# The last GpSimd products and sums of a hybrid diffusion backbone move to VectorE and ScalarE

## The chip, the core and the metric

The kernel runs on one core of a Trainium2 chip. The metric is the device time of one execution in microseconds (us); lower is better. A core has a matrix engine, TensorE (PE in the profile, with PEld for its weight loads), and three engines for the rest: VectorE (DVE), ScalarE (ACT) and GpSimd (POOL). SyncE (SP) issues DMAs, and so do the queues of ACT and POOL. Each engine executes its own queue in order; semaphores make it wait for the others.

## What is computed

One latent sequence and one context sequence of 256 tokens each, 2048 wide, fp32, go through two layers. The even layer runs 8 gated-DeltaNet heads (GDN) in both directions beside 8 neighbourhood-attention heads (NA); the odd layer is a gated short convolution; each is followed by a SwiGLU. The parts that the change touches, cut:

```python
def gated_delta_chunked(q, k, v, g, beta, s0):
    gc = jnp.cumsum(g, axis=-1)
    decay = jnp.exp(jnp.where(lower_incl, gc[..., :, None] - gc[..., None, :], -jnp.inf))
    m = jnp.where(i[:, None] > i[None, :], jnp.einsum('bhnid,bhnjd->bhnij', kb, k) * decay, 0.0)
    t_inv = lax.linalg.triangular_solve(eye + m, ...)
    ...                                        # scan over chunks with state s
def even_mixer(h, hc, ...):
    ka, va, kb, vb, a, b, qa, qb, za = split_segments(h @ w_in, EVEN_SEGS)
    ka, va, qa = short_conv_silu([ka, va, qa], conv_w)
    k_l = axial_rope(l2norm(heads(ka)))
    q_l = axial_rope(l2norm(heads(qa))) * HEAD_DIM ** -0.5
    o_l, _ = gdn_bidirectional(q_l, k_l, heads(va), g_l, beta_l, s_ctx_fin)
    y_gdn = rmsnorm(o_l, gdn_norm) * silu(za)
    y_na = neighbourhood_attention(qb, kb, vb, k_ctx_na, v_ctx_na, rpb)   # scores + rpb, masked
    return concatenate([y_gdn, y_na]) @ w_out
# every layer: x = x + gate * mixer(modulate(x)); x = x + gate * swiglu(modulate(x)); last: rmsnorm
```

## The kernel before

All weights stay in HBM and are streamed. `load_w` (L220) issues 512 KB loads on SP's queue; `split_w` (L229) makes of each 128x1024 block a rounded part whi on ACT (L168) and the rest wlo on DVE (L234); PE then does three products for each block (`tm_stream`, L273 to L276 and L282 to L284, with tokens in the rows; `fm_stream`, L298 and L302, with features in the rows and 256 columns per matmul). A stream that runs on time keeps PE busy; a whi or wlo that is late stops it.

The order of the streams in the even layer is: key blocks KA0 and KA1 (both sequences), query blocks QA0 and QA1, value blocks VA0 and VA1, then QB0 and QB1, KB and VB of the NA heads, and ZA. Between their matmuls stands the GDN work. A finished key, query or value block goes through `head_evac` (L550): a short convolution by four DVE taps and ACT's silu (cv, L535 to L548), transposes into out_t (hq), squares and their sums (L573 to L576). Then `normalise` (L587) scales and rotates keys and queries, and DMAs write them to kd, qTd and vd in HBM. `chunk_matrices` (L772) loads kd again as ktok, takes Gram matrices, multiplies with the exponentials that `decay` (L750) makes of gm, and solves 31 steps of small triangular systems on DVE (L825 and L827), ending in the copy lsol (L828), which goes out as dz (L834). `inverses` (L837 on) reads dz back as xd and xdT (L852) and puts the blocks together on PE (L868 on). `scan`, `latent_scores` (L970 on) and `latent_out` (L992 on) follow. For the NA heads, `na_scores` (L1060) loads a bias br (one buffer, two DMAs on ACT's queue), adds the mask in bq (L1072), takes scores on PE, their maximum on DVE (L1081), the exponential s on ACT (L1083) and the division on DVE (L1084, L1085); `na_values` uses s. Projections are copied by `stage` through nst (L1038) to HBM. `za_evac` (L1104) multiplies the gate with the norm's gain, `resid_evac` (L1134) adds a stream's result to the residual xs, with `norm_h` behind it. The pump's jobs (`ada_job`, L309) run beside all this: DVE sums 512-wide blocks of the modulation weights in acc (L321).

The program order of each engine is not that of the text: a scheduler reorders the instructions of all engines by its own model of their durations, so that a different engine for some operations also moves others.

Of the kernel before, what the change touches and what calls it, by code (L numbers as in the profile page):

```python
# [23 lines left out]
F32 = mybir.dt.float32  # L24
F32R = mybir.dt.float32r
AF = mybir.ActivationFunctionType
OP = mybir.AluOpType
# [77 lines left out]
def body(tc, x, c, ctx, c_ctx, ada_w, ada_b, norm_mix, norm_ffn, ffn_w_gate, ffn_w_up, ffn_w_down,  # L105
# [71 lines left out]
    def C(n):  # L177
        o, w = CO[n]
        return cs[:, o:o + w]
# [370 lines left out]
    def head_evac(n, q, c0, done, sums):  # L550

        st_ = {}

        def f(i_, p):
            st_[i_] = kvp.tile([128, 512], F32, name="hst", tag="hst", bufs=4)[:, 0:n * 128]
            copy(st_[i_], p[:, 0:n * 128])
            if i_ < 3:
                return
            out_t = kvp.tile([128, 4, 4, 128], F32, name="hq", tag="hq", bufs=2)
            ss = kvp.tile([128, 4, 4], F32, name="hss", tag="hss", bufs=2) if sums else None  # L560
            cvs = {}

            def front(i):
                cvs[i] = conv_silu(st_[i], n // 2, c0 + q * 4 + i)

            def back(i):
                pt = smt()
                for t in range(n):
                    ins = transpose(pt[:, t * 128:(t + 1) * 128], cvs[i][:, t * 128:(t + 1) * 128])
                    if not t:  # L570
                        tc.keep_in_program_order(ins)
                acopy(out_t[:, 0:n, i, :], pt[:, 0:n * 128].rearrange("p (t e) -> p t e", t=n))
                if sums:  # L573
                    sq = kvp.tile([128, 4, 128], F32, name="sq", tag="cv", bufs=CV)[:, 0:n, :]
                    POOL.tensor_tensor(sq, out_t[:, 0:n, i, :], out_t[:, 0:n, i, :], op=OP.mult)
                    DVE.tensor_reduce(ss[:, 0:n, i], sq, axis=AX.X, op=OP.add)  # L576


            for g_, i in ((front, 0), (front, 1), (front, 2), (back, 0), (front, 3), (back, 1), (None, 0), (back, 2), (back, 3)):
                if g_:  # L580
                    defer(g_, i)
                else:
                    defer(lambda: None)
            defer(done, out_t, ss)
        return f

    def normalise(xt, n, rs_):  # L587

        for t in range(n):
            xv = xt[:, t]  # L590
            POOL.tensor_tensor(xv, xv, rs_[:, t, :, None].to_broadcast([128, 4, 128]), op=OP.mult)
            if t < 2:
                x1, x2 = xv[:, :, 0:64], xv[:, :, 64:128]
                cb = cosT[:, None, t * 64:(t + 1) * 64].to_broadcast([128, 4, 64])
                sb = sinT[:, None, t * 64:(t + 1) * 64].to_broadcast([128, 4, 64])
                r = kvp.tile([128, 2, 4, 64], F32, name="rope", tag="rope", bufs=1)
                POOL.tensor_tensor(r[:, 0], x1, sb, op=OP.mult)
                POOL.tensor_tensor(r[:, 1], x2, sb, op=OP.mult)
                POOL.tensor_tensor(x1, x1, cb, op=OP.mult)
                POOL.tensor_tensor(x2, x2, cb, op=OP.mult)  # L600
                DVE.tensor_tensor(x1, x1, r[:, 1], op=OP.subtract)
                DVE.tensor_tensor(x2, x2, r[:, 0], op=OP.add)

# [146 lines left out]
    def decay(d, tt, q):  # L750

        gm = g2("gm")
        POOL.tensor_tensor(gm, C(("gt", "lt")[d])[:, None, :].to_broadcast([128, 4, 128]),
                           g_t[:, d, tt, q * 4:q * 4 + 4, None].to_broadcast([128, 4, 128]), op=OP.mult)
        pD = gdt()
        for i in range(4):
            PE.matmul(pD[:, i * 128:(i + 1) * 128], gm[:, i, :], C(("le", "ge")[d]), start=True, stop=True)
        em = g2("em")
        ACT.activation(em, pD.rearrange("p (i e) -> p i e", i=4), AF.Exp)
        return em  # L760
# [208 lines left out]
    def latent_scores(q):  # L969

        qT = load_feat("qT", qTd[:, q * 4:q * 4 + 4, :], lg, 1)
        kT = load_feat("kT", kTd[:, 0, q * 4:q * 4 + 4, :])
        AT = lg.tile([128, 16, 128], F32, name="AT", tag="AT", bufs=2)
        for ti in range(2):
            tok = slice(ti * 128, ti * 128 + 128)
            pK = gdt()
            for i in range(4):
                PE.matmul(pK[:, i * 128:(i + 1) * 128], kT[:, i, tok], qT[:, i, tok], start=True, stop=True)
            for d in range(2):
                em = decay(d, ti, q)  # L980
                POOL.tensor_tensor(em, em, C(("le", "ge")[d])[:, None, :].to_broadcast([128, 4, 128]), op=OP.mult)
                DVE.tensor_tensor(AT[:, d * 8 + ti * 4:d * 8 + ti * 4 + 4, :],
                                  pK.rearrange("p (i e) -> p i e", i=4), em, op=OP.mult)
        return AT
# [8 lines left out]
    def latent_out(q, o_t):  # L993
        zq = load_tok("vtok", zd.rearrange("p t (h e) -> p t h e", h=8), 0, q).rearrange("p t h e -> p t (h e)")
        sso = gw.tile([128, 2, 4], F32, name="sso", tag="sso", bufs=1)
        for t in range(2):
            sq = g2("osq")
            POOL.tensor_tensor(sq, o_t[:, t], o_t[:, t], op=OP.mult)
            DVE.tensor_reduce(sso[:, t], sq, axis=AX.X, op=OP.add)
        ro = rstd(gw, sso, [128, 2, 4], 8, HD, "ro")  # L1000
        for t in range(2):
            for i in range(4):
                DVE.scalar_tensor_tensor(o_t[:, t, i, :], o_t[:, t, i, :], ro[:, t, i:i + 1],
                                         zq[:, t, i * 128:(i + 1) * 128], op0=OP.mult, op1=OP.mult)
        for g in range(2):
            pt = gdt()
            for i in range(2):
                for t in range(2):
                    transpose(pt[:, i * 256 + t * 128:i * 256 + (t + 1) * 128], o_t[:, t, g * 2 + i, :])
            split(yhi[q][:, g * 2:g * 2 + 2, :], ylo[q][:, g * 2:g * 2 + 2, :], pt.rearrange("p (i e) -> p i e", i=2))  # L1010
# [50 lines left out]
    def na_scores(h):  # L1061
        kb = nap.tile([128, 512], F32, name="kb", tag="kb", bufs=2)
        qb = nap.tile([128, 256], F32, name="qb", tag="qb", bufs=2)
        bq = nap.tile([128, 6, 64], F32, name="bq", tag="bq", bufs=2)
        br = nap.tile([128, 6, 64], F32, name="br", tag="br", bufs=1)
        for half in range(2):
            src = bass.AP(tensor=ev_rpb.tensor, offset=ev_rpb.offset + h * 465 + (5 - half) * 31 + 15 - 63,
                          ap=[[1, 64], [31, 6], [1, 64]])
            ACT.dma_start(br[half * 64:half * 64 + 64], src)
        SP.dma_start(kb, kb_d[:, h, :])  # L1070
        SP.dma_start(qb, qb_d[:, h, :])
        POOL.tensor_tensor(bq, br, bandf[:, None, :].to_broadcast([128, 6, 64]), op=OP.add)  # L1072
        out_ = []
        for t in range(2):
            p = nat(h)
            PE.matmul(p, qb[:, t * 128:(t + 1) * 128], kb, start=True, stop=False)
            PE.matmul(p[:, 0:256], C("flip"), bq[:, 2 - 2 * t:6 - 2 * t, :].rearrange("p s c -> p (s c)"),
                      start=False, stop=True)
            s = nap.tile([128, 512], F32, name="s", tag="s", bufs=4)
            m = nap.tile([128, 1], F32, name="m", tag="m", bufs=4)  # L1080
            DVE.tensor_reduce(m, p, axis=AX.X, op=OP.max, negate=True)  # L1081
            l = nap.tile([128, 1], F32, name="l", tag="l", bufs=4)
            ACT.activation(s, p, AF.Exp, bias=m, accum_out=l)  # L1083
            DVE.reciprocal(l, l)  # L1084
            DVE.tensor_scalar(s, s, l, None, op0=OP.mult)  # L1085
            out_.append(s)
        return out_
# [16 lines left out]
    def za_evac(ti, n, p):  # L1104
        o = nsp.tile([128, 512], F32, name="zst", tag="nst", bufs=NST)
        ACT.activation(o, p, AF.Silu)
        ov = o.rearrange("p (h e) -> p h e", h=4)
        POOL.tensor_tensor(ov, ov, gnb[:, None, :].to_broadcast([128, 4, 128]), op=OP.mult)
        ACT.dma_start(zd[:, ti, n * 512:(n + 1) * 512], o)

    held = na_scores(0)
# [21 lines left out]
    def resid_evac(row, c0, gain=None):  # L1133
# [4 lines left out]
        def f(ti, n, p):  # L1138
# [1 line left out]
            v = xs[:, ti, col]  # L1140
            tmp = rpool.tile([128, 512], F32, name="rtmp", tag="rtmp", bufs=2)
            DVE.tensor_tensor(tmp, p, row[:, col], op=OP.mult)
            eng = DVE if c0 and n else POOL
            eng.tensor_tensor(v, tmp, v, op=OP.add)
            ACT.activation(jk, v, AF.Square, accum_out=ssx[:, ti, col.start // 512:col.start // 512 + 1])
            if gain is not None:
                eng.tensor_tensor(v, v, gain[:, col], op=OP.mult)
        return f

    def norm_h(hi, lo, sc_, sh_):  # L1150
# [234 lines left out]
```

## Time and profile before

| | us |
|---|---|
| median of 3 runs (lowest, highest) | 2882.37 (2876.82, 2885.06) |
| the profiled execution | 2891.65 |
| its span, first to last instruction | 2889.6 |
| PE busy in the span | 2747.0 |
| DVE, ACT busy | 1896.9, 1263.6 |

The profile is of one execution, so its durations belong to the 2891.65 us and not to the median. Busy shares say how much an engine does, not who sets the end; for that the table by stretch (busy time of each engine, with its instructions in brackets, the granted clock, the DMA share and GB/s) and the list of waits (engine and line that waited, engine and line that released it, total us, times, longest) are read together. In a timeline a row is start, duration, engine, line, operation, out<-in, and in brackets the idle time before it with what ended it.

### The profile page before, as it was taken

How to read it: one execution, taken by the hardware profiler on the slowest of the kernel's cores; microseconds unless marked ns; L12 is line 12 of the kernel's file. 1: busy time of each engine (PE TensorE's matmuls, PEld its weight loads, DVE VectorE, ACT ScalarE, POOL GpSimd, SP SyncE). 2: the span in 40 equal slices, each digit the busy share in tenths (PEclk: the TensorE clock that was granted, in tenths of full speed). 3: DMA queues.
4: the chain of work that ended last, by engine and by line, in shares of the span. 5: the costliest groups of instructions: out<-in, count | busy, mean ns of one | idle time of the engine just before them, and what ended most of it. 6: DMA issues, size and time to landing. Idle time of an engine off the chain costs nothing.

```text
span 2889.6 us, 40293 instructions
## 1 busy us (share of the span) xinstructions
PE 2747.0 (95%) x15113; PEld 2297.8 (80%) x15113; DVE 1896.9 (66%) x2513; ACT 1263.6 (44%) x1720; POOL 216.0 (7%) x215
## 2 busy tenths in 40 slices
PE   5899989989899899999999999999999999999997
PEld 3699989878777788888888887878878888888886
DVE  3377767755557788766777758787678544445675
ACT  3245534222354444444445554353544444444554
POOL 0025202102010100000000000000000000000010
PEclk9999999989999999999999999999999999999999
DMA  9954567776756698977887766988569766666663
GB/s 342 300 171 133 145 205 252 242 216 193 221 176 224 215 336 318 330 266 273 308 277 265 230 190 239 336 310 298 178 206 327 241 182 183 190 188 216 192 191 123
DMA packets 284927, 680.78 MB, mean 236 GB/s; under 512 B 57274, under 2 KB 97314, under 8 KB 283324
## 3 DMA queue, kind: packets, MB, share of 16 engines
q1 hardware_dynamic: 262148, 652.48, 68.7%
q10 hardware_dynamic: 22583, 25.73, 2.9%
q8 instruction: 118, 1.93, 0.3%
q14 instruction: 78, 0.63, 0.1%
HBM read 657.63 MB, written 20.48 MB: 235 GB/s over the span
## 4 chain that ended last, share of the span: by engine, by line
PE 74%; DMA 12%; DVE 7%; issue 2%; ACT 2%; POOL 1%; SPq 1%; ACTq 0%; DVEq 0%; POOLq 0%
PE mm L273 19%; PE mm L274 19%; PE mm L276 19%; DMA araw<-in_ada_w_dram 7%; PE mm L302 6%; DVE wlo L234 2%; PE mm L282 2%; PE sm L187 2%; PE mm L284 2%; PE mm L283 2%; DVE acc L321 2%; DMA br<-in_ev_rpb_dram 1%; PE gd L466 1%; DMA acc<-in_ada_b_dram 1%; DMA kb_d<-nst 0%
## 5 line engine op out<-in xcount | busy, mean ns | idle before, releaser
L234 DVE TENSOR_TENSOR wlo<-raw,whi 128x1024 fp32r<-128x1024 f32 x800 | 982.9, 1235 | 494.0 <-ACT whi L168 484.7
L168 ACT ACTIVATE whi<-raw 128x1024 fp32r<-128x1024 f32 x800 | 842.4, 1059 | 926.4 <-PE mm L276 668.4
L321 DVE SCALAR_TENSOR_TENSOR acc<-araw,cT,acc 128x1024 f32<-128x1024 f32 (+1 forms) x416 | 437.2, 1051 | 244.0 <-DMA araw<-in_ada_w_dram 222.4
L274 PE MATMUL mm<-wlo,fhi 128*128 128x512 f32 x1232 | 476.9, 393 | 1.0 <-DVE wlo L234 1.0
L273 PE MATMUL mm<-whi,fhi 128*128 128x512 f32 x1232 | 475.8, 396 | 0.0
L276 PE MATMUL mm<-whi,flo 128*128 128x512 f32 x1232 | 391.5, 392 | 0.0
L274 PEld LDWEIGHTS mm<-wlo,fhi 128*128 128x128 f32 x1232 | 232.0, 188 | 50.0 <-DVE wlo L234 1.5
L276 PEld LDWEIGHTS mm<-whi,flo 128*128 128x128 f32 x1232 | 231.0, 188 | 50.5
L273 PEld LDWEIGHTS mm<-whi,fhi 128*128 128x128 f32 x1232 | 232.1, 188 | 48.9
L273 PE MATMUL mm<-whi,ahi 128*128 128x512 f32 x672 | 261.5, 393 | 0.0
L274 PE MATMUL mm<-wlo,ahi 128*128 128x512 f32 x672 | 260.5, 391 | 0.0
L276 PE MATMUL mm<-whi,alo 128*128 128x512 f32 x672 | 210.3, 393 | 0.0
L302 PE MATMUL mm<-hllo,whi 128*128 128x256 f32 x640 | 185.5, 294 | 0.0
L302 PE MATMUL mm<-hlhi,wlo 128*128 128x256 f32 x600 | 171.0, 293 | 3.2 <-DVE wlo L234 3.2
L302 PE MATMUL mm<-hlhi,whi 128*128 128x256 f32 x600 | 169.9, 294 | 1.4 <-DVE hlhi L491 1.0
L171 ACT ACTIVATE ahi<-prodT 128x256 fp32r<-128x256 f32 x176 | 73.2, 417 | 193.7 <-PE mm L274 186.5
L274 PEld LDWEIGHTS mm<-wlo,ahi 128*128 128x128 f32 x672 | 126.2, 188 | 27.7
L276 PEld LDWEIGHTS mm<-whi,alo 128*128 128x128 f32 x672 | 126.1, 188 | 27.5
L273 PEld LDWEIGHTS mm<-whi,ahi 128*128 128x128 f32 x672 | 126.2, 188 | 27.0
L274 PE MATMUL mm<-wlo,dhi 128*128 128x512 f32 x336 | 128.3, 395 | 0.0
L302 PEld LDWEIGHTS mm<-hllo,whi 128*128 128x128 f32 x640 | 127.9, 200 | 0.6
L273 PE MATMUL mm<-whi,dhi 128*128 128x512 f32 x336 | 126.7, 397 | 1.5 <-ACT u_t L168 1.2
(393 smaller groups left out, 4144.0 us busy)
## 6 DMA issues: line engine op xcount, KB each, us to landing
araw<-in_ada_w_dram SPq DMA_DIRECT2D x288, 512.0 KB
raw<-in_ffn_w_down_dram SPq DMA_DIRECT2D x176, 512.0 KB
raw<-in_ffn_w_gate_dram SPq DMA_DIRECT2D x160, 512.0 KB
raw<-in_ffn_w_up_dram SPq DMA_DIRECT2D x160, 512.0 KB
raw<-in_ev_w_in_dram SPq DMA_DIRECT2D x112, 512.0 KB
araw<-in_ada_w_dram SPq DMA_DIRECT2D x192, 256.0 KB
raw<-in_od_w_in_dram SPq DMA_DIRECT2D x96, 512.0 KB
raw<-in_ev_w_out_dram SPq DMA_DIRECT2D x32, 512.0 KB
```

The lines of the kernel that those rows point to most:

```text
L168: ACT.activation(dst, src, AF.Copy)
L171: ACT.activation(hi, src, AF.Copy)
L187: return PE.transpose(dst, src, ident[:n, :n])
L234: DVE.tensor_tensor(lo, raw, hi, op=OP.subtract)
L273: PE.matmul(ps[ti][n], a, hi[:, n * 512:(n + 1) * 512], start=first, stop=False)
L274: PE.matmul(ps[ti][n], a, lo[:, n * 512:(n + 1) * 512], start=False, stop=False)
L276: PE.matmul(ps[ti][n], b, hi[:, n * 512:(n + 1) * 512], start=False, stop=last)
L282: PE.matmul(ps[ti][n], lh(t), hi[:, c_], start=False, stop=False)
L283: PE.matmul(ps[ti][n], lh(t), lo[:, c_], start=False, stop=False)
L284: PE.matmul(ps[ti][n], ll(t), hi[:, c_], start=False, stop=hi is group[-1][0])
L302: PE.matmul(ps[f][:, n * 256:(n + 1) * 256], wt, mv(w, k), start=False, stop=i == len(ks) - 1 and g == len(group) - 1 and j == 2 and w == ...
L321: DVE.scalar_tensor_tensor(acc, raw, cT[:, k:k + 1], acc, op0=OP.mult, op1=OP.add)
```

## The change

Every remaining product or sum of two tensors leaves POOL. In `head_evac` the square of POOL and the reduction of DVE become one ACT instruction for each 128x128 block, which squares and sums; the same in `latent_out`. In `normalise` the scale of 128x512 becomes four ACT copies with a scale, and the rotation's products go to DVE. gm of `decay`, em of `latent_scores`, bq, zst and the residual's adds and final factors go to DVE. POOL goes from 220 instructions to 81, ACT from 1763 to 1872, DVE from 2515 to 2601; PE and SP keep their numbers. ACT's table loads go from 35 to 32. Lines after L591 stand one further down in the new kernel.

```diff
                 if sums:
-                    sq = kvp.tile([128, 4, 128], F32, name="sq", tag="cv", bufs=CV)[:, 0:n, :]
-                    POOL.tensor_tensor(sq, out_t[:, 0:n, i, :], out_t[:, 0:n, i, :], op=OP.mult)
-                    DVE.tensor_reduce(ss[:, 0:n, i], sq, axis=AX.X, op=OP.add)
+                    sq = kvp.tile([128, 128], F32, name="sq", tag="sq", bufs=1)
+                    for t in range(n):
+                        ACT.activation(sq, out_t[:, t, i, :], AF.Square, accum_out=ss[:, t, i:i + 1])
...
-            POOL.tensor_tensor(xv, xv, rs_[:, t, :, None].to_broadcast([128, 4, 128]), op=OP.mult)
+            for i in range(4):
+                ACT.activation(xv[:, i, :], xv[:, i, :], AF.Copy, scale=rs_[:, t, i:i + 1])
...
-                POOL.tensor_tensor(r[:, 0], x1, sb, op=OP.mult)
-                POOL.tensor_tensor(r[:, 1], x2, sb, op=OP.mult)
-                POOL.tensor_tensor(x1, x1, cb, op=OP.mult)
-                POOL.tensor_tensor(x2, x2, cb, op=OP.mult)
+                DVE.tensor_tensor(r[:, 0], x1, sb, op=OP.mult)
+                DVE.tensor_tensor(r[:, 1], x2, sb, op=OP.mult)
+                DVE.tensor_tensor(x1, x1, cb, op=OP.mult)
+                DVE.tensor_tensor(x2, x2, cb, op=OP.mult)
...
-        POOL.tensor_tensor(gm, C(("gt", "lt")[d])[:, None, :].to_broadcast([128, 4, 128]),
+        DVE.tensor_tensor(gm, C(("gt", "lt")[d])[:, None, :].to_broadcast([128, 4, 128]),
...
-                POOL.tensor_tensor(em, em, C(("le", "ge")[d])[:, None, :].to_broadcast([128, 4, 128]), op=OP.mult)
+                DVE.tensor_tensor(em, em, C(("le", "ge")[d])[:, None, :].to_broadcast([128, 4, 128]), op=OP.mult)
...
-            POOL.tensor_tensor(sq, o_t[:, t], o_t[:, t], op=OP.mult)
-            DVE.tensor_reduce(sso[:, t], sq, axis=AX.X, op=OP.add)
+            for i in range(4):
+                ACT.activation(sq[:, i, :], o_t[:, t, i, :], AF.Square, accum_out=sso[:, t, i:i + 1])
...
-        POOL.tensor_tensor(bq, br, bandf[:, None, :].to_broadcast([128, 6, 64]), op=OP.add)
+        DVE.tensor_tensor(bq, br, bandf[:, None, :].to_broadcast([128, 6, 64]), op=OP.add)
...
-        POOL.tensor_tensor(ov, ov, gnb[:, None, :].to_broadcast([128, 4, 128]), op=OP.mult)
+        DVE.tensor_tensor(ov, ov, gnb[:, None, :].to_broadcast([128, 4, 128]), op=OP.mult)
...
-            eng = DVE if c0 and n else POOL
-            eng.tensor_tensor(v, tmp, v, op=OP.add)
+            DVE.tensor_tensor(v, tmp, v, op=OP.add)
             ACT.activation(jk, v, AF.Square, accum_out=ssx[:, ti, col.start // 512:col.start // 512 + 1])
             if gain is not None:
-                eng.tensor_tensor(v, v, gain[:, col], op=OP.mult)
+                DVE.tensor_tensor(v, v, gain[:, col], op=OP.mult)
```

The order of the engines moves with it, at three places above all. ACT's queue at the second key block, before (kd is the DMA behind the normalised keys, whi belongs to the running stream):

```order
L168 ACTIVATE whi<-raw 128x1024
L168 ACTIVATE hq<-sm 128x2x128
L212 ACT_TABLE_LOAD
L212 ACTIVATE rqs<-rqv 128x8
L168 ACTIVATE whi<-raw 128x1024
L615 DMA kd<-hq 512x1x512
```

and now:

```order
L592 ACTIVATE hq<-hq,rkr 128x128 x16
L168 ACTIVATE hq<-sm 128x2x128
L168 ACTIVATE whi<-raw 128x1024
L168 ACTIVATE hq<-sm 128x2x128
L168 ACTIVATE whi<-raw 128x1024
L163 ACTIVATE hst<-mm 128x256
L576 ACTIVATE sq,hss<-hq 128x128
L163 ACTIVATE hst<-mm 128x256
L168 ACTIVATE whi<-raw 128x1024
L616 DMA kd<-hq 512x1x512
```

The scale of the keys stands in this queue now, 16 copies in a row, and the kd DMA comes ahead of the table load for the next square root instead of behind it.

DVE's queue at the end of the first triangular solve (steps L825 and L827, the copy lsol), before:

```order
L234 TENSOR_TENSOR wlo<-raw,whi 128x1024
L825 TENSOR_TENSOR sub_tmp<-lsol,zsol 128x31
L827 TENSOR_TENSOR zsol<-zsol,sub_tmp 128x31
L828 COPY lsol<-zsol 128x1024
L347 COPY g_89<-sm 128x4
L234 TENSOR_TENSOR wlo<-raw,whi 128x1024 x2
L321 SCALAR_TENSOR_TENSOR acc<-araw,cT,acc 128x512 x6
```

and now:

```order
L826 TENSOR_TENSOR sub_tmp<-lsol,zsol 128x31
L545 SCALAR_TENSOR_TENSOR cv<-hst,evcT,cv 128x2x254
L828 TENSOR_TENSOR zsol<-zsol,sub_tmp 128x31
L545 SCALAR_TENSOR_TENSOR cv<-hst,evcT,cv 128x2x255
L545 SCALAR_TENSOR_TENSOR cv<-hst,evcT,cv 128x2x254
L829 COPY lsol<-zsol 128x1024
L545 SCALAR_TENSOR_TENSOR cv<-hst,evcT,cv 128x2x255
L165 COPY hst<-mm 128x512
```

The copy stood behind the last convolution of the value blocks and stands among its first taps now. On PE, the first matmul that uses xd (L869 now, L868 before) stood in QB0 and stands ahead of the last value transposes (L187) now:

```order
L302 MATMUL mm<-hllo,whi 128x256
L869 MATMUL gd<-xd,n_2256 32x32
L187 MATMUL sm<-cs,cv 128x128 x4
L302 MATMUL mm<-hlhi,wlo 128x256 x4
L302 MATMUL mm<-hlhi,whi 128x256
```

Those transposes and the first QB0 matmul stand further apart than before.

DVE's queue at an NA head, before:

```order
L1081 TENSOR_REDUCE m<-sm 128x1
L234 TENSOR_TENSOR wlo<-raw,whi 128x1024
L1084 RECIPROCAL l<-l 128x1 x2
L1085 TENSOR_SCALAR s<-s,l 128x512 x2
L234 TENSOR_TENSOR wlo<-raw,whi 128x1024
```

and now:

```order
L1082 TENSOR_REDUCE m<-sm 128x1
L1085 RECIPROCAL l<-l 128x1
L1073 TENSOR_TENSOR bq<-br,cs 128x384
L1086 TENSOR_SCALAR s<-s,l 128x512
L1085 RECIPROCAL l<-l 128x1
L1086 TENSOR_SCALAR s<-s,l 128x512
L951 TENSOR_TENSOR o_t<-o_t,gd 128x512
L234 TENSOR_TENSOR wlo<-raw,whi 128x1024
```

The next head's bq, which waits for the br DMA, stands between the divisions of this head, with a wlo behind them.

## Rows read from the trace of the kernel before

**Rows 1.** The page, part 1: busy us, share of the span, instructions.

```profile
PE 2747.0 (95%) x15113; PEld 2297.8 (80%) x15113; DVE 1896.9 (66%) x2513; ACT 1263.6 (44%) x1720; POOL 216.0 (7%) x215
```

**Rows 2.** Stretches: length, busy PE, PEld, DVE, ACT, POOL; clock, DMA share, GB/s.

```profile
150.00:950.00 800.00, 732.69 (x5763) 666.62 (x5762) 538.31 (x971) 320.71 (x537) 158.27 (x165) 0.95 0.65 198
350.00:400.00 50.00, 50.00 (x422) 50.00 (x422) 45.18 (x82) 25.58 (x34) 0.00 (x0) 1.00 0.51 154
1000.00:2870.00 1870.00, 1854.99 (x8385) 1520.24 (x8383) 1261.11 (x1336) 875.12 (x1079) 44.90 (x36) 1.00 0.74 247
```

**Rows 3.** Waits of PE, 150 to 950 us: total us, times, longest.

```profile
PE gd L868 <- DMA xd<-dz: 11.1, 4, 6.5
PE mm L298 <- ACT nst L1038: 7.9, 1, 7.9
PE sm L327 <- DVE acc L321: 6.7, 6, 2.2
PE mm L273 <- DVE nst L165: 6.5, 2, 3.9
PE mm L273 <- ACT whi L168: 5.4, 1, 5.4
...
PE sm L187 <- ACT s L1083: 3.9, 1, 3.9
PE sm L187 <- ACT cv L547: 3.3, 3, 1.8
PE mm L302 <- DVE wlo L234: 3.2, 1, 3.2
```

**Rows 4.** POOL's groups by shape: busy us, mean ns | idle before, releaser.

```profile
L1144 POOL TENSOR_TENSOR xs<-rtmp,xs 128x512 f32<-128x512 f32 x24 | 35.9, 1514 | 1086.8 <-DVE rtmp L1142 1051.4 <-DMA araw<-in_ada_w_dram 35.4
```

**Rows 5.** Groups by shape on DVE and ACT, and one timeline row.

```profile
L1142 DVE TENSOR_TENSOR rtmp<-mm,row 128x512 f32<-128x512 f32 x32 | 21.2, 685 | 10.8 <-PE mm L284 7.4 <-POOL xs L1144 3.2
...
L576 DVE TENSOR_REDUCE hss<-sq 128x4 f32<-128x512 f32 x8 | 5.4, 676 | 0.0
...
L602 DVE TENSOR_TENSOR hq<-hq,rope 128x256 f32<-128x256 f32 x8 | 3.3, 416 | 1.6 <-POOL hq L600 1.6
...
L1145 ACT ACTIVATION_READ_ACCUMULATOR jk<-xs 128x1 f32 x32 | 6.0, 186 | 0.0
...
837.51 1.14 ACT L930 ACTIVATE vd<-gd,brest 128x128 f32<-128x128 f32 x4
```

**Rows 6.** Timeline of DVE and POOL at the end of the span.

```profile
2871.41 1.29 DVE L1142 TENSOR_TENSOR rtmp<-mm,row 128x512 f32<-128x512 f32 x2 [4.83 <-PE mm L284]
...
2875.53 1.71 POOL L1144 TENSOR_TENSOR xs<-rtmp,xs 128x512 f32<-128x512 f32 x1
2876.04 1.74 DVE L1144 TENSOR_TENSOR xs<-rtmp,xs 128x512 f32<-128x512 f32 x1
...
2879.80 0.15 DVE L1345 TENSOR_REDUCE ss<-ssx 128x2 f32<-128x8 f32 x1
```

**Rows 7.** Timeline of POOL and ACT at the second key block.

```profile
266.61 6.43 POOL L591 TENSOR_TENSOR hq<-hq,rkr 128x512 f32<-128x512 f32 x4
...
284.48 0.54 ACTq L615 DMA_DIRECT2D kd<-hq  x1
```

**Rows 8.** Timeline of ACT and PE at the start of QB0.

```profile
413.11 0.66 ACT L1038 ACTIVATE nst<-mm 128x256 f32<-128x256 f32 x2 [6.52 <-DMA vd__139<-hq]
...
413.55 0.58 PE L298 MATMUL mm<-h,whi 128*128 128x256 f32 x1 [7.93 <-ACT nst L1038]
```

**Rows 9.** The tile lsol (durations min/median/max, starts), and PE's timeline at xd.

```profile
L828 DVE COPY lsol<-zsol x2: 1075/1088/1102, 400.8 to 599.2; 128x1024 f32<-128x1024 f32 x2
...
616.13 0.28 PE L868 MATMUL gd<-xd,n 32*32 32x32 f32 x2 [6.46 <-DMA xd<-dz]
```

**Rows 10.** POOL's timeline at an NA head, and ACT's wait there.

```profile
781.25 0.99 POOL L1072 TENSOR_TENSOR bq<-br,cs 128x384 f32<-128x384 f32 x1 [10.47 <-DMA br<-in_ev_rpb_dram]
...
ACT s L1083 <- POOL bq L1072: 14.0, 3, 9.6
```

More of the change, by code (lines that the diff above doesn't have):

```diff
@@ L752, in decay @@
         gm = g2("gm")
-        POOL.tensor_tensor(gm, C(("gt", "lt")[d])[:, None, :].to_broadcast([128, 4, 128]),
-                           g_t[:, d, tt, q * 4:q * 4 + 4, None].to_broadcast([128, 4, 128]), op=OP.mult)
+        DVE.tensor_tensor(gm, C(("gt", "lt")[d])[:, None, :].to_broadcast([128, 4, 128]),
+                          g_t[:, d, tt, q * 4:q * 4 + 4, None].to_broadcast([128, 4, 128]), op=OP.mult)
         pD = gdt()
```

## The prediction

> **What bounds the kernel now.** I read the page first: TensorE (PE) is busy in 95% of the span and POOL in 7% [rows 1]. The table by stretch then parts the kernel in two [rows 2]. From 1000 to 2870 us, PE idles for 1870 − 1854.99 = 15 us, and POOL works for 45 us in all: little can be won there. From 150 to 950 us, PE idles for 800 − 732.69 = 67 us, POOL is busy for 158 us, and the granted clock has a mean of 0.95 instead of 1. If the change moves the time, it does so here, where the GDN chain and the NA heads run between the weight streams.
>
> What PE waits for in that stretch comes next [rows 3]. No entry names POOL. The long ones are two DMA round trips (xd from dz, 11.1 us; the staging copy nst behind a vd DMA, 7.9 us), VectorE's acc and nst copies (6.7 and 6.5), whi (5.4), the exponential s (3.9), cv (3.3) and wlo (3.2). So POOL delays PE only through chains: normalise, which ends in the kd and qTd DMAs, and bq ahead of s. A faster product on another engine gives time back only where such a chain ends at a wait of rows 3.
>
> **The change part by part.** The POOL instructions that move are about 167 of POOL's 216 us [rows 1]; its largest form is the residual add, 24 at 1.514 us [rows 4]. What remains on POOL is memsets and small copies.
>
> What VectorE (DVE) takes on. A 128x512 product of two tensors costs 0.685 us there (L1142), a 128x256 one 0.416 (L602) [rows 5]. Added: decay's gm 24 × 0.685 = 16.4; rope 32 × 0.416 = 13.3; em 8 × 0.685 = 5.5; bq 8 × 0.55 = 4.4 (128x384, between the two prices); zst 4 × 0.685 = 2.7; residual adds 24 × 0.685 = 16.4; fn factors 6 × 0.685 = 4.1: 63 us. Removed: the 16 reductions of squares, 8 of them at 0.676 us [rows 5], the rest no longer, so 9 to 11 us. DVE also gets back what it loses beside POOL: its add at 2876.04 us took 1.74 us while POOL's add ran from 2875.53 for 1.71 us [rows 6], against 0.685 for L1142 [rows 5], so at most 1.05 us per POOL instruction of that length. Over 167 us of POOL time, with DVE busy in 67% of the stretch [rows 2], that is at most 167 × 0.67 × 1.05/1.71 = 69 us. Many of DVE's instructions read PSUM or one tensor, and whether those are held as well I can't read from one pair; I take a third to a half, 23 to 34, between ends of 0 and 69. Net load: 63 − 10 − 30 = about +20 us of DVE over 2890, ends −16 and +54. Where DVE has idle time this costs nothing; at 350 to 400 us it has little, 45.18 us busy of 50 [rows 2].
>
> What ScalarE (ACT) takes on: 48 scale copies and 64 squares of 128x128. Its scaled copy of that shape takes 1.14/4 = 0.285 us (L930); a square with its sum adds a read of 0.186 (L1145) [rows 5]. That is 48 × 0.285 + 64 × 0.285 to 0.475 = 32 to 44 us, on an engine that is busy for 321 of 800 us [rows 2]. I put it at nothing: whi, the next in its queue, is made well ahead of PE save in one place (5.4 us in rows 3). If that cover fails, a burst of 16 copies holds whi up for 4.6 us.
>
> The normalise chain. For the second key block, POOL starts the scale at 266.61 us, with 6.43 us for four instructions, then the rope products between squares of other heads, and the kd DMA issues at 284.48 [rows 7]: 17.9 us. After: 16 × 0.285 = 4.6 on ACT, half of it before the first rope, then 12 DVE instructions at 0.416 = 5.0: 7 to 10 us if little is queued between them. So 8 to 11 us of chain vanish in each key block. Few waits hang directly on it; the instruction order already spends the gain by standing the GDN blocks some 11 to 22 us of PE work earlier among the streams. I take −2 us here, from cv and wlo (6.5 us in rows 3), with ends 0 and −6.5.
>
> The end of the value streams. Before, ACT's staging copy nst waits 6.52 us for the vd DMA up to 413.11 us, and PE stalls 7.93 us at QB0's matmul at 413.55 [rows 8]. In that stall the round trip from lsol's copy (400.8 us, 1.09 long) through dz to xd goes unseen. The second such copy ends at 599.2 + 1.09 = 600.3, and PE gets xd at 616.13, after a stall of 6.46 us [rows 9]: a round trip of about 16 us. In the new order the lsol copy stands ahead of the last conv work and not behind it, the last transposes stand earlier than the first QB0 matmul by 13 us of PE work instead of 5 (counted along PE's order, at the 50/422 = 0.12 us a matmul of the stretch from 350 to 400 us in rows 2), so the vd/nst stall of 7.9 us should go. But the inverse's first matmul on xd now stands only some 5 us of PE work behind that lsol copy, and the round trip of 16 us is in the open: a stall of 16 − 5 = 11 us at worst, some 8 if the solve runs ahead. What is late next is therefore xd. Net −7.9 + 8 = 0; ends −8 and +11.
>
> The NA heads. bq waits for the br DMA: POOL sat idle 10.47 us before the one at 781.25 us, and ACT's s waited on bq for up to 9.6 us [rows 10], of which PE paid 3.9 [rows 3]. In the new order the exponentials of the head before stand ahead of the next br issue, so that I take −2.5 of the 3.9. But POOL had nothing else to do while it waited; DVE executes in order, and behind bq now stand wlo and s, for which the streams and na_values wait. br has one buffer, so its load can't start earlier. I add +1.5, with ends 0 and +12.
>
> The rest. zst in za_evac is a product of 0.685 instead of some 1.3 us ahead of a DMA: −1 of the 5.4 of whi. The tail: from 2871.4 DVE does 4 residual products beside POOL and reaches the last reduction at 2879.80 [rows 6]; after, 12 DVE instructions at 0.66 = 7.9 us come from 2871.4 to 2879.35: −0.5. The other norm transitions likewise trade two POOL adds at 1.3 to 1.8 in parallel for two DVE adds at 0.69: 0. gm and em: no row of PE waits on them: 0; their end on the slow side is in DVE's load.
>
> Sum: −2 + 0 − 2.5 + 1.5 − 1 − 0.5 = −4.5 us. The profiled execution took 2891.65 us with a span of 2889.6; this gives 2887 and 2885. It lies 9.3 us above the median of the runs shown, 2882.37, to which I carry the same difference: **2878 us**.
>
> A rule of the Trainium skill speaks against such a move. What rows show: POOL's add and DVE's add stretch each other to 1.7 us [rows 6], and DVE is 90% busy where the streams are dense [rows 2]. The page "Perfetto Trace Analysis", section "Optimizing Scalar/DVE Operations", says that work may go from a saturated DVE to ScalarE or GPSIMD, but that DVE and GPSIMD share a port, so that moves between these two might not help. By its first half the change would be slower (the third rival), by its second half it would change little.
>
> **The rivals.** (A) The forecast, 2878: stall exchanged for stall, small gains.
>
> (B) No successor: xd is in time because the solve, no longer beside POOL, ends early enough. Then 7.9 + 3.9 + 3.3 + 3.2 + 1 = 19.3 us go [rows 3], to 2863. For it: the lsol copy is 20 us earlier in the order. Against it: the xd wait of rows 9 exists in just this form.
>
> (B2) Freed VectorE: without POOL beside it, DVE's acc, nst and wlo come in time, 6.7 + 6.5 + 3.2 = 16.4 us [rows 3], to 2866. For it, rows 6; against it, the 63 us of added work. The Trainium skill, "SBUF — State Buffer", section "SBUF: two separate sides", has a GpSimd instruction and a two-input VectorE one exclude each other for their whole length; the pair in rows 6 agrees (1.74 against 0.685 us).
>
> (C) Slower: DVE's queue stands still at bq. Two waits like that of 10.47 us [rows 10], each less the 4.5 us that I take for wlo's lead over PE: 2 × 6 = +12, to 2894. It decides once DVE reaches bq more than 5 us ahead of br's landing; before, POOL reached it 10 us ahead, and DVE has more queued.
>
> (D) Slower: the new xd stall of 8 to 11 us comes while nst's stays, since the vd DMA shares its queues with the dz ones: +10, to 2892.
>
> **How the numbers follow.** Chances: A 0.42, B 0.27, B2 0.09, C 0.14, D 0.08. About 0.3% (8.6 us) is what a measurement of this kernel can tell from no change: faster means under 2873.7, slower over 2891.0. B and B2 are faster, C and D slower, A within: 0.36, 0.42, 0.22. A's own ends are 2868 to 2890. The range of 2854 to 2896 takes in B with 9 us beyond it (if half-clock stretches behind the stalls go too, as the 0.95 in rows 2 says there are) and C.
>
> **What would show it.** In the new profile POOL is busy about 50 us, DVE's busy time up by some 20 and ACT's by 30 to 45; kd issues 7 to 10 us behind its first scale copy; the nst wait at QB0's start is gone and a wait of gd on xd of about 8 us stands a little earlier; s waits less on bq, now from DVE; the final reduction starts about 8 us after the last residual product began. I am wrong if PE's waits from 150 to 950 us shrink by over 10 us or grow, if DVE waits on br for more than 5 us with PE behind it, or if the time after 1000 us moves by more than 3 us.

## The result: 40 us faster, and the profile after

The changed kernel takes 2844.46 us (median of 4 runs, 2842.9 to 2849.31) against 2883.72 us of the kernel before in the same comparison: a ratio of 0.9861, with a 95% interval of 0.9845 to 0.9877, so 35 to 45 us less. The forecast was 2878 with a range down to 2854. It was wrong by 34 us, on the side of the rivals B and B2 and beyond both.

The page's first part, of the kernel after (it answers to [rows 1]: busy us, share of the span, instructions):

```profile
PE 2726.7 (96%) x15113; PEld 2281.4 (80%) x15113; DVE 1902.5 (67%) x2599; ACT 1292.9 (45%) x1893; POOL 51.0 (2%) x77
```

POOL fell to 51 us as forecast and ACT rose by 29, just under the forecast 30 to 45. VectorE took on 63 us of work, lost 11 of reductions, and is busy for only 5.6 us more, so by this balance about 46 us came back to it: more than the 30 that I took, inside the ends of 0 and 69. The two profiled executions differ by 46.9 us in span, 7.6 more than the medians, mainly because the profiled execution of before took 2891.65 us, more than its median. What follows splits the 46.9.

To see where it goes, both traces are cut where the weight streams have done the same number of matmuls (750, 1500, 2560, 3072, 3328, 3584 and 4000 of 11880; W_out's stream is the matmuls 3625 to 4008, so that the last cut lies at its very end). Columns as in [rows 2]; first the kernel before:

```profile
0.00:196.10 196.10, 158.52 (x1154) 119.28 (x1155) 84.53 (x173) 59.96 (x85) 17.84 (x20) 0.97 0.86 282
196.10:328.00 131.90, 121.93 (x988) 119.47 (x987) 98.09 (x198) 76.08 (x120) 57.38 (x66) 0.97 0.47 144
328.00:502.50 174.50, 162.49 (x1734) 158.30 (x1733) 129.42 (x221) 71.38 (x107) 23.81 (x32) 0.96 0.70 210
502.50:636.80 134.30, 120.88 (x972) 108.68 (x972) 88.01 (x189) 37.40 (x76) 13.18 (x16) 0.92 0.78 235
636.80:711.30 74.50, 64.51 (x603) 57.32 (x602) 38.71 (x50) 15.74 (x23) 15.96 (x14) 0.86 0.62 183
...
825.30:984.10 158.80, 144.40 (x681) 115.65 (x680) 106.44 (x174) 72.61 (x112) 22.74 (x17) 0.97 0.68 226
984.10:2889.60 1905.50, 1869.57 (x8449) 1532.16 (x8447) 1285.18 (x1392) 890.65 (x1113) 51.67 (x41) 0.99 0.73 244
```

and the kernel after:

```profile
0.00:191.30 191.30, 155.51 (x1154) 117.48 (x1155) 86.20 (x183) 70.94 (x135) 4.74 (x8) 0.99 0.90 293
191.30:315.00 123.70, 119.67 (x989) 118.09 (x988) 91.56 (x215) 90.62 (x213) 8.81 (x18) 0.99 0.51 154
315.00:485.60 170.60, 164.11 (x1757) 160.33 (x1757) 132.75 (x240) 75.03 (x119) 12.91 (x22) 0.98 0.70 215
485.60:621.60 136.00, 122.44 (x1219) 109.94 (x1218) 90.84 (x182) 37.62 (x73) 7.94 (x9) 0.95 0.76 231
621.60:676.50 54.90, 53.52 (x371) 49.18 (x370) 41.01 (x59) 14.12 (x21) 1.05 (x2) 1.00 0.77 244
...
787.30:938.00 150.70, 140.13 (x641) 110.55 (x640) 103.37 (x171) 72.98 (x130) 1.06 (x2) 0.98 0.70 233
938.00:2842.70 1904.70, 1867.44 (x8449) 1530.43 (x8447) 1285.92 (x1420) 890.92 (x1113) 14.01 (x16) 0.99 0.73 245
```

Behind the last cut nothing moves: 1905.5 against 1904.7 us. Up to there PE does the same 15113 − 8449 = 6664 matmuls in 984.1 us before and in 938.0 after. It is busy for 2746.96 − 1869.57 = 877.4 us of them before and for 859.2 after. So of the 46 us, 28 are less waiting (106.7 to 78.8 us) and **18 are the same matmuls done faster**: behind stalls PE ran for some microseconds at the lower clock, and the granted clock rises from 0.92 and 0.86 to 0.95 and 1.00 in the two stretches where the second set of inverses ran. The clock records of the two traces agree: up to the last cut 92 us passed at the lower level (1.2 GHz of 2.4) before and 41 after, and PE was busy for 79 and 39 of these, so that half of the 40 us less, about 20, is matmul time given back. The two stretches of the second inverses together shrink by 17.9 us, the second row (in which the second key block is scaled and rotated) by 8.2, the last one, most of it W_out's stream, by 8.1, and the one in which PE stalled on nst before (third row) by 3.9.

PE's waits in the changed kernel from 150 to 950 us (as in [rows 3]):

```profile
PE sm L187 <- DVE xc L1159: 6.3, 1, 6.3
PE mm L298 <- DVE nst L165: 5.3, 1, 5.3
...
PE mm L273 <- ACT whi L168: 3.8, 2, 3.5
PE sm L187 <- ACT cv L547: 3.1, 2, 1.8
PE sm L1078 <- DVE bq L1073: 2.8, 1, 2.8
PE gd L869 <- issue: 2.5, 1, 2.5
...
PE mm L298 <- ACT nst L1039: 2.0, 1, 2.0
...
PE mm L302 <- DVE wlo L234: 0.8, 2, 0.5
```

The xc of the first entry belongs to the norm behind W_out, which ran after 950 us before. The 11.1 us on xd are gone, and only 2.5 us with no named releaser stand at the first matmul on xd. The 7.9 us on nst are gone from where they stood, but 5.3 and 2.0 us on nst stand at later streams now; all waits on nst together fall from 14.7 us (7.9, 6.5 and 0.3) to 7.7. s (3.9) and qb (4.2) have given way to bq (2.8).

A name has to be set right here. What the rows and the prediction call QB0's matmul at 413.55 us [rows 8] is the first of QB1's stream: QB0's begins at 379.85 us, and the nst that is late there holds QB0's results. Likewise the first matmul on xd stood in QB1's stream before (418.33 us) and stands in QB0's now (375.75 us). The distances that the prediction counts to that matmul are right.

```profile
379.85 0.28 PE L298 MATMUL mm<-h,whi 128*128 128x256 f32 x1
```

### The profile page after: what moved, and what is told of

It reads as the page before. It is cut to its first block, busy times and chain, and to the rows that moved or that the text cites. A ratio compares the mean times of both kernels' runs of the same rounds, so it can differ in the third digit from the quotient of the medians.

```text
span 2842.7 us, 40317 instructions
## 1 busy us (share of the span) xinstructions
PE 2726.7 (96%) x15113; PEld 2281.4 (80%) x15113; DVE 1902.5 (67%) x2599; ACT 1292.9 (45%) x1893; POOL 51.0 (2%) x77
## 4 chain that ended last, share of the span: by engine, by line
PE 66%; DMA 18%; DVE 10%; issue 3%; ACT 2%; SPq 1%; POOL 0%; ACTq 0%; DVEq 0%; POOLq 0%
PE mm L276 16%; PE mm L273 16%; PE mm L274 16%; DMA araw<-in_ada_w_dram 12%; PE mm L302 8%; DVE acc L321 3%; DVE wlo L234 3%; PE sm L187 2%; PE mm L282 2%; PE mm L284 2%; PE mm L283 2%; DMA br<-in_ev_rpb_dram 1%; DMA acc<-in_ada_b_dram 1%; DMA raw<-in_od_w_in_dram 1%; PE gd L466 1%
## 5 line engine op out<-in xcount | busy, mean ns | idle before, releaser
L234 DVE TENSOR_TENSOR wlo<-raw,whi 128x1024 fp32r<-128x1024 f32 x800 | 972.3, 1222 | 476.0 <-ACT whi L168 463.7
L321 DVE SCALAR_TENSOR_TENSOR acc<-araw,cT,acc 128x1024 f32<-128x1024 f32 (+1 forms) x416 | 431.2, 1037 | 229.7 <-DMA araw<-in_ada_w_dram 196.3
```

The source lines that it names most:

```text
L234: DVE.tensor_tensor(lo, raw, hi, op=OP.subtract)
L321: DVE.scalar_tensor_tensor(acc, raw, cT[:, k:k + 1], acc, op0=OP.mult, op1=OP.add)
```

## Experiments: which part

Each kernel is compared with the kernel before on the same chip; "us" is one less the ratio, times 2884, with the 95% interval in the same way. An edit named "x stays" or "x moves" is just that line of the diff that is shown above the prediction, in the one kernel or the other.

**Each part alone.** The kernel before with squares, scale and rotation of keys and queries moved:

> Before, with only the squares, the scale and the rotation of keys and queries (head_evac, normalise) moved off POOL. Chain theory (the gain is the shorter normalise chain, which lets the GDN blocks run earlier so that nst and xd are no longer waited for): -25 to -35 us of the -39, the wait of PE on xd (11.1 us) and on nst (7.9) both gone. Port theory (DVE gets time back in proportion to the POOL time removed beside it, 60 of 167 us): about -14 us, and both waits of PE shorter but there. Place theory (each part removes the stalls next to it): about -20 us.

Ratio 0.9938 (0.9915 to 0.996): −18 us (−12 to −25). With gm, em and latent_out's squares moved:

> Before, with only gm, em and the squares of latent_out moved. Chain theory: within 5 us of before. Port theory (47 of 167 us of POOL time): about -11 us. Place theory: -5 to -8 us, from the second xd wait.

0.9976 (0.9958 to 0.9995): −7 us. With bq and zst moved:

> Before, with only bq and zst moved. Chain theory: within 5 us of before. Port theory (14 of 167 us): about -3 us. Place theory: -8 to -12 us, since s (3.9), whi behind zst (5.4) and their half-clock stretches go.

1.002 (0.9996 to 1.0044): +6 us, the interval reaching just below zero. With the residual adds and factors moved:

> Before, with only the residual adds and the final factors moved. Chain theory: within 3 us. Port theory (47 of 167 us): about -11 us. Place theory: -1 to -2 us, all of it in the last 20 us and at the transition to the first feed-forward layer.

0.9998 (0.9976 to 1.002): −1 us. POOL's residual work took 47 us, and moving it is worth nothing that can be measured (−7 to +6). That speaks against the port theory in the proportion I gave it. It doesn't show what a freer VectorE would be worth: with the 30 products taken on, it is busy for 1898.6 us in that kernel against 1896.9 before. The sum is −18 − 7 + 6 − 1 = −20, give or take some 13: about half of the 40 us isn't in any single part.

**The whole change less one part.** First less the keys' and queries' part:

> The whole change less its part on keys and queries (squares, scale and rotation stay on POOL). If the parts add up as they measured alone (-18, -7, +6, 0): about -2 us against before. If the parts need each other (chain theory: the other parts pay only once the keys are early): the same, 0 to -2. If every part frees its share of one resource (port theory): about -25 us.

0.9981 (0.9959 to 1.0004): −5 us. Less the GDN products:

> The whole change less gm, em and the squares of latent_out. Added up from the single parts: -13 us against before. If the -20 that the single parts leave unexplained come from keys and GDN together (both on the path from kd to xd): about -13 too, that is, all of the surplus goes with this part. If the surplus comes from keys with bq or zst: about -33 us.

0.9911 (0.9878 to 0.9944): −26 us. Less bq and zst:

> The whole change less bq and zst. Added up: -26 us against before. If bq on DVE costs 6 us in the whole change as it did alone: faster than the whole change, -46. If the surplus comes from the NA heads (nothing but memsets left on POOL there): about -20.

0.9889 (0.9859 to 0.9919): −32 us. Less the residual:

> The whole change less the residual adds and factors. Place theory: within 2 us of the whole change, -38 to -40 against before. If the scheduler's order upstream depends on it: anything down to -25.

0.9886 (0.9855 to 0.9918): −33 us. So the keys' part is the condition: without it the rest gives 5 us (not clear of zero), with it the rest gives another 22. The losses of the other three are 14, 8 and 7 us. Each of these three runs has an interval of some 9 us to either side, so that the first loss is just clear of it and the last two are not.

**Inside the keys' part.** The whole change less its squares:

> The whole change less the squares of keys and queries (POOL's product and DVE's reduction stay). If the squares carry the keys' 34 us: about -6 us against before. If scale and rotation carry them: -35 to -40. In proportion to POOL's time on that path (squares 15 of 60 us): about -31.

0.9893 (0.9873 to 0.9913): −31 us. Less scale and rotation:

> The whole change less scale and rotation (they stay on POOL). If the squares carry the keys' 34 us: -35 to -40 us against before. If scale and rotation carry them: -6 to -10. In proportion to POOL's time: about -14.

0.9989 (0.9975 to 1.0004): −3 us. Less the scale alone:

> The whole change less the scale in normalise (12 POOL products of 128x512 stay). Chain theory: the scale is 6.4 of 17.9 us of the keys' chain, against 4.6 on ACT, so little is lost: -30 to -38 us against before. If the chain isn't it and POOL's time counts (16.5 of the 45 us in normalise): -27.

0.9897 (0.9879 to 0.9915): −30 us. Less the rotation alone:

> The whole change less the rotation's products (32 of 128x256 stay on POOL). Chain theory: the rotation is the long end of the keys' chain (16 products at 0.73 us, 11.7 us, with two DVE steps between, against about 5): most of the 36 us of normalise go with it, -5 to -15 us against before. If POOL's time counts (28 of 45 us): -17.

0.9945 (0.9928 to 0.9963): −16 us. Without scale and rotation 37 of the 40 us are gone, 24 with the rotation alone, 10 with the scale alone. The rotation has the larger part, as by the chain; its −16 lies between the two theories' numbers and doesn't tell them apart.

## Experiments: order or engines

The scheduler reorders all engines when one operation becomes faster. To part the two effects, the orders of PE, SP, DVE and ACT were written into the other kernel as edges without a wait, for all instructions that both have:

```diff
+def hold_order(nc, tc):
+    bb = list(nc.cur_bb.bb.instructions)
+    for e, text in ORDER.items():           # the other kernel's order, packed
+        mine = [i for i in bb if str(i.engine) == "EngineType." + e]
...
+        for p, q in zip(at, at[1:]):
+            tc.add_manual_dep(mine[q], mine[p].name, ...NoSync...)
...
         body(tc, *args)
+        hold_order(nc, tc)
```

The old engines in the new order:

> The kernel before with every product on its old engine, but PE, SP, DVE and ACT hold the instruction order of the changed kernel (the squares' tile sq has a buffer of its own instead of one of cv's, so that this order has no circular wait). Order theory (the gain is the place of the GDN blocks in the queues, which the scheduler moved ahead because it believed the keys to be ready sooner): -20 to -40 us against before. Duration theory (the gain is that the keys are in truth ready sooner, and an order alone buys nothing): 0 to +30 us, since PE then reaches the GDN blocks before POOL's normalise has fed them, with waits on ktok and hq of 5 to 15 us each.

0.9932 (0.9907 to 0.9956): −20 us (−13 to −27). **The order alone gives half of the gain**, with POOL as busy as before (213 us). (The buffer of its own for sq, which this run needs, was not tried without the order.) The first solve's copy lsol starts at 379.7 us in it, against 400.8 before and 366.55 in the changed kernel. The new engines in the old order:

> The changed kernel with its engines, but PE, SP, DVE and ACT hold the order of the kernel before for all instructions that both have. Duration theory: -20 to -30 us against before, since nst and xd come sooner by the 8 to 11 us that normalise saves. Order theory: within 10 us of before, since the stalls sit where the order puts them (nst behind the vd DMA at the start of QB0, xd behind the second solve).

0.9966 (0.9948 to 0.9985): −10 us (−4 to −15). In the old order nst and xd stand where they stood, and the first lsol copy starts at 398.7 us. PE's waits on them in that kernel, 150 to 950 us:

```profile
PE mm L298 <- ACT nst L1039: 8.4, 1, 8.4
...
PE gd L869 <- DMA xd<-dz: 7.7, 4, 3.5
```

These are the 7.9 us of [rows 3] and 7.7 of the 11.1 us on xd (the longest fell from 6.5 to 3.5), though the products are as short there as in the changed kernel: the 16 copies of the second key block take 4.79 us against 4.80. But the old order puts other work between them and keeps the kd DMA behind the table load, so that kd issues 20.3 us after the first copy (258.29 to 278.63), later than the 17.9 us of before. So these stalls belong mostly to the order; and this run doesn't show what keys that are in truth ready sooner would be worth, since the order kept them from being sent.

Part of what the new order lacks with the old engines shows at the second key block and the first query block. A timeline of VectorE there, with PE's row, in the kernel with the old engines in the new order:

```profile
259.87 0.42 DVE L576 TENSOR_REDUCE hss<-sq 128x2 f32<-128x256 f32 x1 [1.51 <-POOL sq L575]
264.43 0.42 DVE L576 TENSOR_REDUCE hss<-sq 128x2 f32<-128x256 f32 x1 [4.14 <-POOL sq L575]
266.51 0.93 DVE L601 TENSOR_TENSOR hq<-hq,rope 128x256 f32<-128x256 f32 x1 [1.66 <-POOL hq L599]
...
269.97 0.93 DVE L601 TENSOR_TENSOR hq<-hq,rope 128x256 f32<-128x256 f32 x1 [1.86 <-POOL hq L599]
...
271.49 3.48 DVE L234 TENSOR_TENSOR wlo<-raw,whi 128x1024 fp32r<-128x1024 f32 x3
...
272.75 1.22 PE L302 MATMUL mm<-h,wlo 128*128 128x256 f32 x4 [6.76 <-DVE wlo L234]
```

VectorE stands in its queue on what POOL has yet to make, the square's product and the rotation, and behind these stand three wlo of the running stream; PE, which needs the first of them, stalls 6.76 us. POOL appears in no list of PE's waits in this stretch: it holds PE up through VectorE's queue. VectorE's waits for POOL between matmuls 750 and 1500 are in all:

```profile
DVE hq L601 <- POOL hq L599: 9.8, 4, 4.2
DVE hss L576 <- POOL sq L575: 7.8, 4, 4.1
```

in the old engines' kernel, and none in the changed one. That stretch takes 135.1 us in the one and 123.7 in the other. Next, within the new order, scale and rotation alone were moved, and all the others without these two:

> The order of the changed kernel on PE, SP, DVE and ACT, with scale and rotation of normalise on ACT and DVE and every other product on POOL as before (sq with a buffer of its own). If the 20 us that the order alone leaves are PE's waits for POOL's normalise at the key blocks: about -31 to -36 us against before. If they are POOL in VectorE's way in general, or the other parts: -20 to -25.

0.9866 (0.984 to 0.9891): −39 us (−31 to −46).

> The order of the changed kernel, with everything but scale and rotation moved (these stay on POOL). If normalise holds the remainder: about -20 to -25 us against before, as with the order alone. If the other parts hold it: -35 to -40.

0.9883 (0.9853 to 0.9913): −34 us (−25 to −42). In the new order, scale and rotation alone reach the changed kernel's time; but so nearly do the other parts, which I had put at −20 to −25 if normalise held the remainder. It doesn't hold it alone. Nor do VectorE's waits for POOL explain both: in the stretch above they fall from 17.6 us to 2.1 in the first of the two runs, but only to 14.6 in the second, where PE still stalls 5.6 us on wlo. The intervals of some 8 us to either side are too wide to share out the last 20 us further.

The second run has a twin. It is the whole change less scale and rotation (−3 us, −7 to +1), with nothing added but the held order: **the same engines, in the order of the changed kernel instead of the one that the scheduler chose for them, are about 30 us faster.** Its first lsol copy starts at 377.2 us against 396.3, though POOL does the same work in both. PE's wait at the first matmul on xd, in the twin with the scheduler's own order and then with the held one, is

```profile
PE gd L868 <- issue: 10.5, 1, 10.5
...
PE gd L868 <- issue: 3.8, 2, 2.8
```

So with all the others moved, most of what moving scale and rotation brings (some 30 of 37 us) is the order that the scheduler then chooses.

## Experiments: is it the keys' DMA?

If what counts is when kd is written, it can be written earlier with POOL left as it is: the context tiles need no rotation, and the first chunk_matrices needs only them.

```diff
-            normalise(kt, 4, rstd(kvp, ss, [128, 4, 4], 16, 1.0, "rk"))
-            ACT.dma_start(hslice(kd, 0, 4, q), kt.rearrange("p t h e -> p t (h e)"))
+            rk = rstd(kvp, ss, [128, 4, 4], 16, 1.0, "rk")
+            for t0 in (2, 0):
+                normalise(kt, 4, rk, (t0, t0 + 1))
+                ACT.dma_start(hslice(kd, t0, 2, q), kt[:, t0:t0 + 2].rearrange("p t h e -> p t (h e)"))
```

In the kernel before:

> The kernel before, all products on POOL, but normalise takes the two context tiles of the keys first (they need no rotation) and sends them to kd by a DMA of their own, so that the first chunk_matrices need not wait for the rotation. Chain theory (what counts is when kd is there): -15 to -30 us against before, with POOL as busy as before. Engine theory (what counts is that POOL is out of VectorE's way or that VectorE and ScalarE are faster at each product): within 5 us of before.

0.9964 (0.995 to 0.9979): −10 us (−6 to −14), with the wanted DMA issued at 270.8 us instead of 284.48 [rows 7] and the solve's copy at 372.4 instead of 400.8 [rows 9]. Less than the chain theory's −15, more than the engine theory's 5. VectorE's waits for POOL at the key blocks stay in it:

```profile
DVE hq L601 <- POOL hq L599: 6.6, 4, 2.2
DVE hss L576 <- POOL sq L575: 6.4, 2, 5.9
```

So an earlier kd goes with a part of the gain. The scheduler reordered this kernel too, so the run doesn't part the earlier kd from the order that came with it, and that POOL in front of VectorE's queue withholds the rest is argued, not shown. In the changed kernel:

> The changed kernel with the same split of the keys' normalise. Chain theory: another 3 to 8 us below the changed kernel, -43 to -48 against before (the rotation of one key block, some 5 to 6 us on DVE, leaves the path). Engine theory: as the changed kernel, -38 to -42.

0.9859 (0.9841 to 0.9876): as fast as the changed kernel, not measurably faster. There kd comes hardly sooner (258.7 instead of 259.46 us); the first lsol copy starts 6 us sooner (360.2), and the time doesn't follow. No version here beats the change.

## Why the prediction was wrong, point by point

**The step that failed first** is the end of the normalise chain: "Few waits hang directly on it; the instruction order already spends the gain", and −2 us. The order was treated as a place where a gain vanishes. It is the larger part of the gain: the order alone gives 20 us with the old engines and 30 with all the others moved. With the GDN blocks earlier PE's waits on xd fall from 11.1 us to 2.6 and those on nst from 14.7 to 8.1 in the old engines' kernel, where the forecast had the one grow by what the other lost; the two stretches of the second inverses, for which the sum has no term, are 15.0 us shorter there, the one of the stall on nst only 1.6. Scale and rotation, priced at −2, carry 37 of 40 us when taken out of the whole change. The chain's own price was about right: the second key block's scale starts at 253.47 us and kd issues at 259.46:

```profile
253.47 4.80 ACT L592 ACTIVATE hq<-hq,rkr 128x128 f32<-128x128 f32 x16 [1.07 <-DVE rkr L216]
...
259.46 0.55 ACTq L616 DMA_DIRECT2D kd<-hq  x1
```

that is 6.0 us against 17.9 before (for the first key block 10.4), where 7 to 10 were forecast.

**The term that was mis-sized** is the successor of nst at the value streams' end, +8 us of xd. I took the dz round trip as 16 us from the second solve, where PE stood waiting for it. After, the first solve's copy ends at 366.55 + 1.13 = 367.7 us and PE has xd at 375.75:

```profile
366.55 1.13 DVE L829 COPY lsol<-zsol 128x1024 f32<-128x1024 f32 x1
...
375.75 0.28 PE L869 MATMUL gd<-xd,n 32*32 32x32 f32 x2 [2.45 <-issue]
```

8.1 us, half as long, and a stall of 2.45. The outgoing half makes most of the difference: in the kernel before, POOL's memset of xd waited for the dz DMA, issued at 600.26 us, until 608.71 us, 8.4 us; in the changed kernel it started at 371.77, 4.1 us after the issue at 367.70. Behind the dz issue of before SP's queue had two adaptive-weight loads; that these slowed it is not shown.

```profile
600.93 5.68 SPq L320 DMA_DIRECT2D araw<-in_ada_w_dram  x2
...
608.71 0.95 POOL L846 MEMSET xd<- 128x1024 f32 x1 [16.61 <-DMA dz<-zsol]
...
611.90 0.86 SPq L852 DMA_DIRECT2D xd<-dz  x2
```

The round trip was read off one place where somebody waits for it, and of the two it was the longer. A stall of the forecast's size did come, in another kernel: the 10.5 us on xd of the change less scale and rotation in its own order.

**What no term held**: the clock. All stalls were priced at their idle time; 18 of the 46 us are the same matmuls, fewer of them at the lower clock. The prediction mentions it only for the edge of the range. In [rows 2] the 0.95 stood there to be used: in a ten-us piece behind the 6.46 us stall of [rows 9] the kernel before shows a mean granted clock of 0.59, in one around the next xd stall of 0.56:

```profile
616.00:626.00 10.00, 8.75 (x220) 8.18 (x221) 3.76 (x7) 2.49 (x5) 0.00 (x0) 0.59 0.92 237
640.00:650.00 10.00, 8.34 (x93) 7.69 (x93) 2.80 (x4) 1.44 (x2) 1.31 (x2) 0.56 0.55 168
```

**What was not seen**: VectorE's in-order queue was feared for bq, behind br. It was already held up in that way by POOL, and the change ends that; what this alone is worth stays open. L602's row in [rows 5], read only for its price, says so with 1.6 us; VectorE's waits in the kernel before, from 150 to 1000 us, say more:

```profile
DVE hq L601 <- POOL hq L599: 7.0, 4, 2.2
```

The rivals B and B2 were also put as alternatives to each other; save for the 3.2 us of wlo, which both count, their 19 and 16 us come from different waits, and 32.5 us is their sum. What B forecast, an xd in time, came, but not for B's reason: with POOL beside the solve as before, the new order alone leaves 2.6 us of that wait.

**What held.** The products cost on VectorE what the rows said (gm 0.685 us, rotation 0.418, bq 0.553). bq on VectorE does wait for br, 12.7 us in all and up to 5.7, of which PE pays 2.8; alone with zst it costs about 6 us (not clear of zero), against the −2 forecast for s, zst and br together. The residual is worth nothing, and the tail from the first residual product to the last reduction falls from 8.39 to 7.55 us (−0.5 forecast). The time behind the last blocks of W_out stayed within 1 us.

**What stays open**: how the 20 us between the old and the new engines in the same order share out, and whether the GDN and NA parts are in truth worth more in the whole change (14 and 8 us) than alone (7 and −6), which the intervals hardly tell. That each part makes the scheduler choose a somewhat different order is a possible cause that was only argued.

## To carry to other kernels

Where a scheduler sets the order, a faster operation changes the places of others, and that can be worth as much as the operation: hold the one order in the other kernel to see which it is. An engine that is absent from the list of waits of the bound engine can still hold it up through a third one's in-order queue: read what that third engine waits for, and what is queued behind. Price a stall with the slow stretch behind it, and a round trip from more than the one place where it was waited for.

## What the runs showed of the hardware

A 128x512 product of two tensors took VectorE 0.685 us in the changed kernel, in each of 24 gm with hardly any POOL work beside it, while the same form took POOL 1.251 us before. By the balance of busy times VectorE got some 46 us of its own time back for about 165 us of POOL time removed. In the residual, whose adds took POOL 1.514 us each [rows 4] and take VectorE 0.682, moving 47 us of POOL's work bought nothing that can be measured (−1 us, −7 to +6): POOL and VectorE had worked there side by side, and PE's waits for the norm behind it are 18.0 us before and 18.5 in the changed kernel.
